# The low parts of the streamed weights on POOL: two instructions of half a tile each in place of one of the whole tile

## Chip, cores and metric

One Trainium2 chip, one of its cores. The metric is the device time of one execution in microseconds (us); lower is better. The times given are medians over runs of the whole kernel. The engines are called PE (matrix multiply; PEld is its weight load), DVE (vector), ACT (scalar), POOL (GpSimd) and SP (the queue that issues the DMAs).

## What is computed

One layer of a bidirectional encoder on 2048 positions of width 1024, in float32: an RMS norm, one projection into attention and state-space inputs, windowed attention beside a two-way state-space scan, an output projection, and a gated feed-forward block with a short convolution. By far the most arithmetic lies in the products with the weights:

```python
def reference(x, ...):
    for l in range(DEPTH):
        h = rmsnorm(x, norm1_g[l])
        proj = h @ w_in[l]
        q, k, v, z, xbc, dt_raw = jnp.split(proj, IN_SPLITS, axis=-1)
        attn = rmsnorm(windowed_attention(q, k, v, ...), attn_out_g[l])
        ssd = ssd_mixer(z, xbc, dt_raw, ...)
        x = x + jnp.concatenate([attn, ssd], axis=-1) @ w_out[l]
        h = rmsnorm(x, norm2_g[l])
        u = dwconv(h @ w_up[l], ffn_conv_w[l], ffn_conv_b[l])
        gate, val = jnp.split(u, 2, axis=-1)
        x = x + (jax.nn.silu(gate) * val) @ w_down[l]
    return rmsnorm(x, final_norm_g)
```

## The kernel before

Every large product is made of three matmuls on float32r operands, since one alone is too coarse: each operand is split into a high part `hi` (rounded to float32r) and a low part `lo` (the rest, `raw - hi`). `mm3` (lines 107 to 109) issues, for one 128 x 128 block of weights and one block of 512 positions, first `whi` with `xhi` (L107), then `whi` with `xlo` (L108), then `wlo` with `xhi` (L109). Only L109 reads the low part of the weights.

The weights stream through the core in 336 tiles of 128 partitions x 1024 columns (768 in some tiles of the down projection). A tile holds eight blocks of 128 columns, used one after the other: `up_mm` runs the eight blocks (index `k`) of one tile in turn, 24 matmuls in all; `wo_unit` does the same for the output projection; in `down_unit` the first half of the tile's columns belongs to one block of output rows and the second half to the next.

`next_w` keeps the stream two tiles ahead. For each tile, `w_raw` issues the DMA into `wraw`, and `w_split` makes `whi` with a copy on ACT (L142) and `wlo` with a subtraction that reads `wraw` and `whi` (L143). That subtraction runs on DVE for 24 tiles of the first stage (the first five and those listed in `WVS`) and on POOL for the other 312. `wraw`, `whi` and `wlo` have two buffers each, so tile i waits for the matmuls of tile i-2 to be done with theirs; for a few tiles `wplace` gives a place of their own (`wup`, `wdn`).

What else POOL does stands in the same queue: the low parts of some activation blocks (`split`, L209), sums of squares (L205), and steps of the state-space scan (L629, L631, L919, L941, L943), nearly all on 512 columns.

The stages: up to about 610 us the projections, scans and first attention blocks, in an order written out by hand (`PLAN`). Then four blocks `j` of 512 positions through the feed-forward part, the last one ending the kernel; beside each of the first three run attention and scan of the next block (`start_side`, `pace`), and between blocks stands the output projection (`wo_split` L991, `wo_x1`, `wo_unit`) with the norm stage `h2_stage`. The program text gives a first order. The builder then schedules the instructions by its own estimate of when each can run, and with that fixes the order of each engine's queue and the semaphore waits.

Of the kernel before, what the change touches and what calls it, by code (L numbers as in the profile page):

```python
# [10 lines left out]
F32 = mybir.dt.float32  # L11
F32R = mybir.dt.float32r
AF = mybir.ActivationFunctionType
ALU = mybir.AluOpType
# [22 lines left out]
WV = 5  # L37
PC = (1, 1, 1)
SQ_LAG = 7
WVS = (2, 3, 4, 6, 7, 9, 10, 12, 13, 14, 19, 21, 25, 26, 27, 28, 29, 31, 32, 33, 36, 40)  # L40
# [17 lines left out]
def block_kernel(ctx: ExitStack, tc: tile.TileContext, a: dict, out: bass.AP):  # L58
# [53 lines left out]
    V, G, A, T = nc.vector, nc.gpsimd, nc.scalar, nc.tensor  # L112
# [7 lines left out]
    def w_raw(i):  # L120
        if i >= len(wplan) or i in wraws:
            return
        src, m = wplan[i]
        raw = wpool.tile([P, 1024], F32, tag="wraw", name="wraw")
        dst = raw[:, :m]
        if len(src.shape) == 3:
            dst = dst.rearrange("p (i n) -> p i n", i=2)
        nc.sync.dma_start(dst, src)
        wraws[i] = raw

    def w_split(i):
        if i >= len(wplan) or i in wdone:
            return
        w_raw(i)
        m = wplan[i][1]
        raw = wraws[i]
        if i in wplace:
            hi, lo = wplace.pop(i)
        else:
            hi = wpool.tile([P, 1024], F32R, tag="whi", name="whi")  # L140
            lo = wpool.tile([P, 1024], F32R, tag="wlo", name="wlo")
        A.copy(hi[:, :m], raw[:, :m])  # L142
        (V if i < WV or i in WVS else G).tensor_tensor(lo[:, :m], raw[:, :m], hi[:, :m].bitcast(F32), ALU.subtract)  # L143
        wdone[i] = (hi, lo)

    def next_w():
        i = wpos[0]
        wpos[0] += 1
        w_split(i)
        w_raw(i + 1)  # L150
        w_split(i + 1)
        w_raw(i + 2)
        return wdone.pop(i)
# [1238 lines left out]
    for j in range(NB):  # L1392
# [5 lines left out]
        for g, (k0, nk) in enumerate(GROUPS):  # L1398
# [3 lines left out]
            i = 0  # L1402
            if j == 0 and g == 0 and UP2:
# [9 lines left out]
                i = 2  # L1413
# [118 lines left out]
```

## Time and profile before

| | before |
|---|---|
| median of 3 runs | 2447.28 us (2445.77 to 2447.74) |
| the profiled execution, device time | 2447.17 us |
| its span, first to last instruction | 2445.0 us |
| granted PE clock, mean | 0.986 of full speed |
| PE busy | 2344.5 us, 96% |
| DVE / ACT / POOL busy | 1666.2 / 1075.4 / 1091.7 us |

PE is the engine with the least idle time. Its busy time is that of overlapping instructions: a matmul of 512 columns is shown with some 0.39 us, while the next one starts 0.23 us after it. The idle time of the weight loads tells more plainly where PE had to stand. A row of the timeline gives start, duration, engine, line, operation, what is written and read, and in brackets the idle time before it and what ended it. Times are in us from the start of the span unless ns is said.

### The profile page before, as it was taken

How to read it: one execution, taken by the hardware profiler on the slowest of the kernel's cores; microseconds unless marked ns; L12 is line 12 of the kernel's file. 1: busy time of each engine (PE TensorE's matmuls, PEld its weight loads, DVE VectorE, ACT ScalarE, POOL GpSimd, SP SyncE). 2: the span in 40 equal slices, each digit the busy share in tenths (PEclk: the TensorE clock that was granted, in tenths of full speed). 3: DMA queues.
4: the chain of work that ended last, by engine and by line, in shares of the span. 5: the costliest groups of instructions: out<-in, count | busy, mean ns of one | idle time of the engine just before them, and what ended most of it. 6: DMA issues, size and time to landing. Idle time of an engine off the chain costs nothing.

```text
span 2445.0 us, 31146 instructions
## 1 busy us (share of the span) xinstructions
PE 2344.5 (96%) x11440; PEld 1955.9 (80%) x11440; DVE 1666.2 (68%) x2867; ACT 1075.4 (44%) x1818; POOL 1091.7 (45%) x585
## 2 busy tenths in 40 slices
PE   7999998897999999999999999999999999999997
PEld 6878797776788878777888887778888877888887
DVE  5756777687886784567877675688676566844445
ACT  5443565345454443435444444354444343433334
POOL 1014314464545544455454454555544445544444
PEclk9999999898999999999999999999999999999998
DMA  6466445883443433333444343244333232423232
GB/s 230 157 202 217 137 147 169 243 289 117 131 138 101 143 125 98 120 93 125 130 139 132 104 136 121 87 134 136 126 126 95 83 126 85 130 95 95 95 93 80
DMA packets 172459, 325.80 MB, mean 133 GB/s; under 512 B 12690, under 2 KB 83730, under 8 KB 172308
## 3 DMA queue, kind: packets, MB, share of 16 engines
q1 hardware_dynamic: 172308, 323.83, 41.5%
q8 instruction: 90, 1.47, 0.3%
q14 instruction: 61, 0.50, 0.1%
HBM read 277.77 MB, written 44.71 MB: 132 GB/s over the span
## 4 chain that ended last, share of the span: by engine, by line
PE 52%; DVE 7%; POOL 3%; DMA 1%; issue 1%; ACT 1%; DVEq 0%; POOLq 0%; ACTq 0%
PE up_b L109 10%; PE up_b L107 10%; PE up_b L108 10%; PE dn_b L107 3%; PE dn_b L109 3%; PE dn_b L108 3%; POOL wlo L143 2%; PE dn L109 2%; PE dn L108 2%; PE dn L107 2%; DVE m_lo L991 1%; PE wo_b L109 1%; DVE sm L777 1%; PE wo_b L108 1%; PE wo_b L107 1%
## 5 line engine op out<-in xcount | busy, mean ns | idle before, releaser
L143 POOL TENSOR_TENSOR wlo<-wraw,whi 128x1024 fp32r<-128x1024 f32 (+1 forms) x306 | 742.5, 2427 | 890.1 <-ACT whi L142 819.0
L142 ACT CAST whi<-wraw 128x1024 fp32r<-128x1024 f32 (+1 forms) x330 | 339.2, 1028 | 558.7 <-PE up_b L108 214.1
L109 PE MATMUL up_b<-h_hi,wlo 128*128 128x512 f32 x1392 | 550.4, 396 | 11.4 <-POOL wlo L143 11.4
L107 PE MATMUL up_b<-h_hi,whi 128*128 128x512 f32 x1392 | 552.0, 397 | 1.1 <-ACT h_hi L208 0.7
L108 PE MATMUL up_b<-h_lo,whi 128*128 128x512 f32 x1392 | 550.3, 396 | 1.9 <-DVE h_lo L209 1.9
L1066 DVE SCALAR_TENSOR_TENSOR fa<-up_b,fcw,fa 128x510 f32<-128x510 f32 (+2 forms) x396 | 271.2, 686 | 246.5 <-ACT fa L1068 242.3
L109 PEld LDWEIGHTS up_b<-h_hi,wlo 128*128 128x128 f32 x1392 | 262.3, 188 | 73.4 <-POOL wlo L143 15.4
L108 PEld LDWEIGHTS up_b<-h_lo,whi 128*128 128x128 f32 x1392 | 262.4, 188 | 59.7 <-DVE h_lo L209 3.5
L107 PEld LDWEIGHTS up_b<-h_hi,whi 128*128 128x128 f32 x1392 | 261.8, 188 | 59.1 <-ACT whi L142 1.2
L107 PE MATMUL dn_b<-f,whi 128*128 128x512 f32 x528 | 211.4, 400 | 1.1 <-DVE hal L1077 0.7
L108 PE MATMUL dn_b<-f,whi 128*128 128x512 f32 x528 | 209.0, 396 | 0.0
L109 PE MATMUL dn_b<-f,wlo 128*128 128x512 f32 x528 | 204.7, 396 | 0.0
L1068 ACT ACTIVATE fa<-up_b,fcw 128x512 f32<-128x512 f32 x176 | 135.9, 774 | 11.4 <-DVE fth L1089 11.1
L1116 DVE TENSOR_TENSOR x<-x,dn_b 128x512 f32<-128x512 f32 x144 | 97.7, 680 | 62.1 <-PE dn_b L109 61.6
L1087 ACT ACTIVATE fth<-fa 128x512 f32<-128x512 f32 (+1 forms) x88 | 55.6, 632 | 164.7 <-DVE fa L1079 115.6
L107 PEld LDWEIGHTS dn_b<-f,whi 128*128 128x128 f32 x528 | 99.7, 189 | 24.1 <-issue 2.1
L894 DVE SCALAR_TENSOR_TENSOR ab<-ab,ldt,mask 128x128 f32<-128x128 f32 x256 | 104.3, 475 | 19.0 <-DMA ab<-acs_d 19.0
L109 PEld LDWEIGHTS dn_b<-f,wlo 128*128 128x128 f32 x528 | 99.4, 188 | 21.9
L108 PEld LDWEIGHTS dn_b<-f,whi 128*128 128x128 f32 x528 | 99.2, 188 | 21.1
L1093 DVE TENSOR_TENSOR f<-fth,f 128x512 fp32r<-128x512 f32 (+1 forms) x88 | 105.7, 1201 | 14.4 <-ACT f L1092 13.5
L1092 ACT CAST f<-fth 128x512 fp32r<-128x512 f32 (+1 forms) x88 | 54.2, 616 | 107.9 <-DVE fth L1089 105.6
L107 PE MATMUL pj_b<-h_hi,whi 128*128 128x512 f32 x208 | 84.9, 409 | 15.1 <-ACT h_hi L236 6.8
(336 smaller groups left out, 4841.0 us busy)
## 6 DMA issues: line engine op xcount, KB each, us to landing
wraw<-in_w_up SPq DMA_DIRECT2D x176, 512.0 KB
wraw<-in_w_dn SPq DMA_DIRECT2D x64, 512.0 KB
wraw<-in_w_out SPq DMA_DIRECT2D x36, 512.0 KB
ab<-acs_d SPq DMA_DIRECT2D x32, 512.0 KB
wraw<-in_w_ch SPq DMA_DIRECT2D x28, 512.0 KB
wraw<-in_w_dn SPq DMA_DIRECT2D x32, 384.0 KB
ak<-ks_d SPq DMA_DIRECT2D x14, 768.0 KB
xt<-in_x SPq DMA_DIRECT2D x16, 512.0 KB
```

The source lines that it names most:

```text
L107: nc.tensor.matmul(ps, whi, xhi, start=first, stop=False)
L108: nc.tensor.matmul(ps, whi, xlo, start=False, stop=False)
L109: nc.tensor.matmul(ps, wlo, xhi, start=False, stop=last)
L142: A.copy(hi[:, :m], raw[:, :m])
L143: (V if i < WV or i in WVS else G).tensor_tensor(lo[:, :m], raw[:, :m], hi[:, :m].bitcast(F32), ALU.subtract)
L894: (G if i < SUBP[0 if first else 1] else V).scalar_tensor_tensor(ab[:, i, d], ab[:, i, d], ldt[:, d, c, h : h + 1], mask3[:, 2 * d * P : ( ...
L1066: V.scalar_tensor_tensor(o, src, w(q), o, ALU.mult, ALU.add)
L1068: A.activation(ai[:, 0:TB], u, AF.Identity, bias=w(3), scale=w(2))
L1087: A.activation(th[:, :n], acc[:, 0, :n], AF.Tanh)
L1092: A.copy(fs[:, idx, 0, :n], th[:, :n])
L1093: V.tensor_tensor(fs[:, idx, 1, :n], th[:, :n], fs[:, idx, 0, :n].bitcast(F32), ALU.subtract)
L1116: V.tensor_tensor(xv, xv, ps[i], ALU.add)
```

## The change

In `w_split`, the tiles whose low part is made on POOL get it in two subtractions, the first over the first half of the columns, the second over the second half (512 each, or 384 each where the tile has 768). Tiles on DVE, the ACT copy and the DMAs are as before.

```diff
         A.copy(hi[:, :m], raw[:, :m])
-        (V if i < WV or i in WVS else G).tensor_tensor(lo[:, :m], raw[:, :m], hi[:, :m].bitcast(F32), ALU.subtract)
+        if i < WV or i in WVS:
+            V.tensor_tensor(lo[:, :m], raw[:, :m], hi[:, :m].bitcast(F32), ALU.subtract)
+        else:
+            for q in range(2):
+                sl = slice(q * m // 2, (q + 1) * m // 2)
+                G.tensor_tensor(lo[:, sl], raw[:, sl], hi[:, sl].bitcast(F32), ALU.subtract)
         wdone[i] = (hi, lo)
```

## Rows read from the trace of the kernel before

**Rows 1.** Page: busy time, share of the span and instructions of each engine.
```profile
PE 2344.5 (96%) x11440; PEld 1955.9 (80%) x11440; DVE 1666.2 (68%) x2867; ACT 1075.4 (44%) x1818; POOL 1091.7 (45%) x585
```
**Rows 2.** Page: the chain that ended last, shares of the span by line.
```profile
PE up_b L109 10%; PE up_b L107 10%; PE up_b L108 10%; PE dn_b L107 3%; PE dn_b L109 3%; PE dn_b L108 3%; POOL wlo L143 2%; PE dn L109 2%; PE dn L108 2%; PE dn L107 2%; DVE m_lo L991 1%; PE wo_b L109 1%; DVE sm L777 1%; PE wo_b L108 1%; PE wo_b L107 1%
```
**Rows 3.** Page, costliest groups: busy us, mean ns, idle before, releaser.
```profile
L143 POOL TENSOR_TENSOR wlo<-wraw,whi 128x1024 fp32r<-128x1024 f32 (+1 forms) x306 | 742.5, 2427 | 890.1 <-ACT whi L142 819.0
...
L109 PEld LDWEIGHTS up_b<-h_hi,wlo 128*128 128x128 f32 x1392 | 262.3, 188 | 73.4 <-POOL wlo L143 15.4
L108 PEld LDWEIGHTS up_b<-h_lo,whi 128*128 128x128 f32 x1392 | 262.4, 188 | 59.7 <-DVE h_lo L209 3.5
```
**Rows 4.** Waits of the weight loads: us in total, times, longest.
```profile
PEld up_b L109 <- POOL wlo L143: 15.4, 10, 3.2
PEld sc L754 <- DVE mxs L756: 11.1, 9, 3.2
PEld pt L782 <- DVE pl L786: 9.2, 3, 3.6
...
PEld wo_b L109 <- POOL wlo L143: 6.8, 8, 2.0
```
**Rows 5.** Timeline, weight loads of L109 that waited.
```profile
1094.58 0.19 PEld L109 LDWEIGHTS up_b<-h_hi,wlo 128*128 128x128 f32 x1 [1.17 <-POOL wlo L143]
...
1102.19 0.19 PEld L109 LDWEIGHTS up_b<-h_hi,wlo 128*128 128x128 f32 x1 [1.79 <-POOL wlo L143]
```
**Rows 6.** Chain of waits in order of time (start, us, what), a block transition.
```profile
1025.86 8.00 DMA x<-in_xT
...
1038.79 0.50 PE wo_b L109
1039.29 0.23 PE wo_b L107
```
**Rows 7.** Durations on POOL, by form (mean ns) and by line (ns min/median/max).
```profile
L143 POOL TENSOR_TENSOR wlo<-wraw,whi 128x1024 fp32r<-128x1024 f32 x278 | 688.4, 2477 | 816.6 <-ACT whi L142 752.2 <-DVE x L1016 12.5 <-PE sc L755 12.1
...
L143 POOL TENSOR_TENSOR wlo<-wraw,whi x306: 1832/2406/4035, 59.7 to 2403.4; 128x1024 fp32r<-128x1024 f32 x139, 128x768 fp32r<-128x768 f32 x14
...
L209 POOL TENSOR_TENSOR h_True_lo<-xb,h_True_hi x8: 1283/1313/1768, 235.0 to 262.0; 128x512 fp32r<-128x512 f32 x8
```
**Rows 8.** Timeline: a first matmul with a tile still being written.
```profile
2053.70 0.39 PE L108 MATMUL up_b<-h_lo,whi 128*128 128x512 f32 x1
...
2058.11 1.31 POOL L209 TENSOR_TENSOR h_lo<-h2t,h_hi 128x512 fp32r<-128x512 f32 x1 [1.28 <-ACT h_hi L208]
```
**Rows 9.** Durations on DVE, by line, by form, and one row of the timeline.
```profile
L777 DVE TENSOR_SCALAR sm<-sm,rsm x96: 346/415/2595, 571.4 to 1894.7; 128x384 f32<-128x384 f32 x88, 128x256 f32<-128x256 f32 x8
...
L777 DVE TENSOR_SCALAR sm<-sm,rsm 128x384 f32<-128x384 f32 x88 | 74.0, 893 | 0.5
...
L1066 DVE SCALAR_TENSOR_TENSOR fa<-up_b,fcw,fa x396: 205/748/754, 653.0 to 2397.3; 128x510 f32<-128x510 f32 x153, 128x511 f32<-128x511 f32 x23, 128x1 f32<-128x1 f32 x22
...
1021.69 2.88 DVE L991 SCALAR_TENSOR_TENSOR m_lo<-mixed,gv,m_hi 128x512 fp32r<-128x512 f32 x1
```
**Rows 10.** Timeline, POOL and DVE side by side.
```profile
1175.86 3.13 POOL L143 TENSOR_TENSOR wlo<-wraw,whi 128x1024 fp32r<-128x1024 f32 x1 [8.25 <-ACT whi L142]
1178.94 1.10 POOL L631 TENSOR_TENSOR statef<-statef,etot 128x512 f32<-128x512 f32 x1
...
1177.24 1.90 DVE L894 SCALAR_TENSOR_TENSOR ab<-ab,ldt,mask 128x128 f32<-128x128 f32 x1
...
1179.06 1.13 DVE L894 SCALAR_TENSOR_TENSOR ab<-ab,ldt,mask 128x128 f32<-128x128 f32 x1
```
**Rows 11.** Timeline: PE's order within one group of three matmuls.
```profile
1203.86 0.40 PE L108 MATMUL up_b<-h_lo,whi 128*128 128x512 f32 x1
...
1204.10 0.27 PE L818 MATMUL apr<-ident,arc 128*128 128x128 f32 x1
...
1204.13 0.48 PE L109 MATMUL up_b<-h_hi,wlo 128*128 128x512 f32 x1
```

## The prediction, made before the result was known

> **What bounds the kernel now.** I read the page's busy shares first: PE has work in 96% of the span, every other engine in less than 70% [rows 1]. PE is the bound, so a change elsewhere pays only where PE stands. The chain that ended last says by whose work PE is reached late: besides PE's own lines the largest entry is POOL's `wlo` on L143 with 2% of the span, some 49 us, then DVE's `m_lo` and `sm` with 1% each, some 24 us each [rows 2]. A share of the chain is not yet a loss, for PE may have been only just late. The loss stands in the waits of the weight loads: those of L109 waited for `wlo` 15.4 us in 10 places of the up projection and 6.8 us in 8 of the output projection, together 22.2 us in 18 stalls, the longest 3.2 us [rows 4]. That is 0.9% of the span and the most that an earlier `wlo` can return directly. The other waits of PE that bear on this are those for DVE: 11.1 us for `mxs`, 9.2 us for `pl` [rows 4].
>
> POOL itself is at 45% [rows 1]; the low parts take 742.5 us of it, and 819.0 of the 890.1 us idle before them ends with the ACT copy of `whi` [rows 3]. So as a rule POOL waits for its input and is late only where other work of its queue, or a late ACT copy, came in between. Of 312 tiles on POOL only some 18 are late for PE; the others have slack, and an earlier or later `wlo` changes nothing there.
>
> **Part 1, the first half comes earlier (the gain).** A `wlo` of 1024 columns takes 2.41 us in the median, 2.48 in the mean; the same subtraction on 512 columns (`h_True_lo`, float32r out as here) takes 1.31 us in the median, 1.28 at the least [rows 7]. PE needs only the first 128 columns of `wlo` for its first L109. If the wait goes by the half, the first L109 of a tile starts 2.41 - 1.31 = 1.10 us earlier.
>
> Does it go by the half? The trace of before shows a tile that is written in pieces: a matmul of L108 on `h_lo` runs at 2053.70, and POOL writes a piece of the same `h_lo` at 2058.11 [rows 8]. So the waits follow the region that an instruction touches, not the whole tile.
>
> When is the second half due? Its first reader is block 4 of the tile, 12 matmuls behind the first L109; at 0.23 us from one matmul to the next [rows 6] that is 2.76 us. It is ready 1.31 us behind the first half, or some 2.0 us if a DVE instruction of 0.7 us gets in between. It is hidden with 0.7 us to spare.
>
> Now the 18 stalls one by one in the timeline: eleven are over 1.1 us and add to 19.1 us, seven are below 0.7 us and add to 3.1 us; two of the eleven are shown [rows 5]. An earlier first half takes 1.10 us from each of the eleven, 12.1 us, and the whole of the seven, 3.1 us: 15.2 us. One deduction: the two shown, 7.6 us apart, repeat in the next block, and in such a pair the second `wlo` stands behind POOL's `h_lo`, whose time PE does not set. What PE gains at the first stall it waits for at the second, so one 1.10 of each pair is lost: 15.2 - 2.2 = **13.0 us gained**. Bounds: 15.2 if the pairs do add, 6.5 (half) if other work is next late.
>
> **Part 2, more waits on PE (at nothing).** Each of the 312 tiles gets a second semaphore wait, on the weight load of block 4. Of the weight loads of the up projection, those of L109 hold the waits for POOL; they take 188 ns like those of L108, and their idle time without the waits named is 73.4 - 15.4 = 58.0 us against 59.7 - 3.5 = 56.2 us over 1392 loads each [rows 3]. The difference is 1.8 us for some 170 satisfied waits, so at most 3 us for 312. A load overlaps the matmul before it, which is the cover; I take 0 and keep 3 for the range.
>
> **Part 3, POOL works longer (a cost).** Two halves take 2 x 1.31 = 2.62 us against 2.41: 0.21 us a tile, 66 us over 312 tiles. If POOL's 2.48 us mean is mostly waiting for DVE at the start, a pair may meet it twice, 0.07 us more. POOL goes from 45% to some 48% of the span; what is queued behind a `wlo` (scan steps, `h_lo`, the next `wlo`) starts 0.2 us later. On the path this counts only where the chain holds a whole `wlo` with more POOL work behind it, as at 1175.86 with `statef` behind [rows 10]. The 49 us of the chain [rows 2] are some 20 tiles, most of them those that PE waits for at once. I take 10 tiles at 0.21: **2 us lost**; bounds 0 and 6 (20 tiles at 0.28).
>
> [...]
>
> **Part 4, DVE is held for less (a gain of unsure size).** DVE's `sm` (L777) has a median of 415 ns but a mean of 893 and a maximum of 2595, that is, its own time plus the length of a `wlo` [rows 9]. `m_lo` took 2.88 us in one row, while L1066, of the same kind and width but fed from PSUM, never took over 754 ns [rows 9]. The place is plain at 1177.24: a small DVE instruction stays 1.90 us, until the `wlo` of 1175.86 ends at 1178.99, and the next stays 1.13 us, until `statef` ends [rows 10]. So a DVE instruction that takes its inputs from SBUF is held while POOL runs one, and POOL's next instruction goes ahead of DVE's next but one. Half of `sm` is such time, some 13 us of its 24 on the chain; for `m_lo` I take the same, 12 us. Halves help a DVE instruction that comes during the first half (one in two): it is let in 1.1 us earlier. If another such one follows at once, the second half holds that one instead, and nothing is won. A quarter of 25 us would be 6; since PE's own waits for DVE here are only 20.3 us [rows 4], **4 us gained**. Bounds: half, 12, and below zero 2 us lost, since a pair is 8% longer than one whole.
>
> [...]
>
> **The sum.** 13.0 + 4 - 2 = 15 us less. The profiled execution took 2447.17 us, with a span of 2445.0 and 2.2 around it; the median shown is 2447.28, the same within 0.1 us. So 2447.2 - 15 = **2432 us**, -0.6%. From the bounds its own range is 2421 to 2442 (15.2 + 12 gained and 1 lost; 13 gained, 2 lost on DVE and 6 on POOL).
>
> **Rivals.**
> (a) The gain is absorbed: PE arrives earlier and stands at the next late thing. For it: 8.00 us of `x<-in_xT` stand on the chain at 1025.86, before the output projection's stall at 1038.79 [rows 6], and DVE paces much of what comes before. Against it: at the 18 stalls it was `wlo` that came last, and the stretches between are PE's own. With half of part 1 and parts 3 and 4 in balance: -6.5, 2441 us.
> (b) The change does not do what it says: L109 waits for both halves after all. Then every stall is longer by 0.21, 18 x 0.21 = 4 us lost, 2 lost on POOL, 4 gained on DVE: 2449 us. Against it stands the `h_lo` written in pieces [rows 8].
> (c) Slower: other POOL work gets between the two halves. The queues are not in the order of the text: a transpose of the attention stands between the second and third matmul of one group [rows 11]. 312 more instructions with other times are scheduled anew. The place is the three blocks with scan steps beside the up projection, as around 1175 [rows 10]. The second half is due 2.76 us behind the first; with one POOL step of 1.3 us and one DVE hold of 0.7 in between it comes at 3.3 and PE stands 0.5 us, with two steps 1.9 us, on average 1.2. From 13 such tiles on the gain of 15 us is gone; with two in each of the 12 scan chunks of these blocks, 24 x 1.2 = 29 us, it is 2461 us. Nothing in the rows shows such an order, but nothing excludes it.
>
> **How the numbers follow.** About 0.2% (5 us) is what a measurement of this kernel can tell from no change. The forecast has 0.54, all of it faster. Rival (a), 2437 to 2446, has 0.22, of which 0.09 are faster by more than 5 us and 0.13 not. Rival (b) has 0.07, no change. Rival (c) has 0.17, slower. Together: faster 0.63, same 0.20, slower 0.17. The range goes from 2418 (the forecast's own low end and 3 us more, for reordering may also help) to 2452, which takes in (a) and (b) and leaves most of (c) out.
>
> **What the profile of the changed kernel would show.** Right: the waits of L109's weight loads for `wlo` fall from 22 to about 8 us, with hardly any at block 4; 624 POOL instructions on L143 with a median near 1.3 us and POOL busy near 1160 us; the mean of `sm` well below 893 ns. Part 1 is wrong if the stalls stay with the releaser being the second half (b), or if PE's idle time before other lines grows by what L109's falls (a). Rival (c) shows as stalls of L109 released by second halves, with other POOL work between the two. What would upset all of it is a visibly different order of PE's queue, with new stalls at lines that this change does not touch.

## The result, and the profile after

The changed kernel takes **2421.11 us** (median of 4 runs, 2418.16 to 2425.67) against 2447.51 us before (4 runs, 2445.77 to 2449.55): 26 us less, and by the estimate over the runs a ratio of 0.9898 [0.9882, 0.9913]. 2432 was forecast, with a range from 2418 to 2452: the sign and the range hold, and the forecast gain of 15 us is too small by 11; the measured time lies at the low end that the prediction's own bounds gave, 2421. The profiled execution of after is its slowest, 2425.67 us with a span of 2423.9. The traces below therefore show 21.1 of the 26 us.

The page of after: busy time, share and instructions of each engine, the chain that ended last by line, and three of the costliest groups (busy us, mean ns, idle before, releaser).

```profile
PE 2341.8 (97%) x11440; PEld 1958.3 (81%) x11440; DVE 1572.2 (65%) x2867; ACT 1076.3 (44%) x1818; POOL 1164.1 (48%) x897
...
PE up_b L109 11%; PE up_b L108 11%; PE up_b L107 11%; PE dn_b L108 5%; PE dn_b L107 5%; PE dn_b L109 5%; POOL wlo L148 2%; PE wo_b L109 2%; PE wo_b L108 2%; PE wo_b L107 2%; PE dn L108 1%; PE dn L107 1%; PE dn L109 1%; PE pt L787 1%; DVE ab L899 1%
...
L148 POOL TENSOR_TENSOR wlo<-wraw,whi 128x512 fp32r<-128x512 f32 (+1 forms) x612 | 815.4, 1354 | 812.0 <-ACT whi L142 757.6
...
L109 PEld LDWEIGHTS up_b<-h_hi,wlo 128*128 128x128 f32 x1392 | 261.6, 188 | 63.7 <-POOL wlo L148 6.9
L108 PEld LDWEIGHTS up_b<-h_lo,whi 128*128 128x128 f32 x1392 | 261.6, 188 | 59.6 <-DVE h_lo L214 3.4
```

Against [rows 1], POOL has 312 more instructions and 72.4 us more work. DVE has the same 2867 instructions and 94.0 us less busy time, although the change adds, removes or alters no DVE instruction. That second difference is the larger surprise of the page; part of it will turn out to belong to the order of the instructions and not to the halves. On the chain, DVE's `m_lo` and `sm`, 1% each in [rows 2], are no longer among the listed lines, and PE's own lines have grown (up projection from 10 to 11% a line, down projection from 3 to 5%). Against [rows 3], the idle time of L109's loads behind `wlo` has fallen from 15.4 to 6.9 us.

The waits of the weight loads after (us in total, times, longest):

```profile
PEld sc L759 <- DVE mxs L761: 9.5, 9, 3.2
PEld pt L787 <- DVE pl L791: 7.4, 3, 4.0
PEld up_b L109 <- POOL wlo L148: 6.9, 9, 1.9
PEld wo_b L109 <- POOL wlo L148: 4.7, 6, 1.1
PEld pj_b L107 <- DVE cu L337: 3.5, 2, 3.2
```

Two rows of the same view of before that [rows 4] does not show:

```profile
PEld pj_b L107 <- DVE cu L332: 7.0, 2, 3.9
PEld po L792 <- DVE pl L786: 3.8, 5, 1.4
```

The two rows on `wlo`, 22.2 us in 18 stalls in [rows 4], are now 11.6 us in 15. In the timeline each of these 15 is released by the first half of its tile, none by the second. The rows for DVE have fallen as well: `mxs` from 11.1 to 9.5, `pl` from 9.2 to 7.4 [rows 4], `cu` from 7.0 to 3.5. Over all lines, the gaps of over 0.1 us before weight loads add to 122.6 us before and 99.6 after (0.044 us, the usual step, taken off each). Of these 23.0 us, 10.9 lie at `wlo` and 12.1 elsewhere, 10.7 of them at loads that wait for DVE (51.2 us before, 40.5 after). So the traces already say that half of the gain is not at the line that the change was aimed at.

Durations after, on POOL and DVE (lines of the source: ns min/median/max; groups by form: busy us, mean ns):

```profile
L148 POOL TENSOR_TENSOR wlo<-wraw,whi x612: 1007/1297/2342, 62.1 to 2383.1; 128x512 fp32r<-128x512 f32 x139, 128x384 fp32r<-128x384 f32 x14
...
L782 DVE TENSOR_SCALAR sm<-sm,rsm x96: 345/417/1484, 572.3 to 1878.8; 128x384 f32<-128x384 f32 x88, 128x256 f32<-128x256 f32 x8
L782 DVE TENSOR_SCALAR sm<-sm,rsm 128x384 f32<-128x384 f32 x88 | 51.9, 643 | 0.4
L996 DVE SCALAR_TENSOR_TENSOR m_lo<-mixed,gv,m_hi x36: 473/804/1780, 522.7 to 1966.3; 128x512 fp32r<-128x512 f32 x28, 128x256 fp32r<-128x256 f32 x8
```

Two halves take 2 x 1.297 = 2.594 us in the median against 2.406 [rows 7]. The longest `sm` went from 2595 to 1484 ns and the mean from 893 to 643 [rows 9]. The longest `m_lo` went from 2887 ns (first row below) to 1780: what it has over the median fell from 2.15 us (740 ns) to 0.98 (804 ns), as a tile's 2.41 us on POOL became a half's 1.30.

The same place in both traces, the output projection's `m_lo` beside two tiles of low parts. The line's durations before, and the timeline of before (start, us, what):

```profile
L991 DVE SCALAR_TENSOR_TENSOR m_lo<-mixed,gv,m_hi x36: 469/740/2887, 521.6 to 1986.4; 128x512 fp32r<-128x512 f32 x28, 128x256 fp32r<-128x256 f32 x8
...
1018.58 5.44 POOL L143 TENSOR_TENSOR wlo<-wraw,whi 128x1024 fp32r<-128x1024 f32 x2 [4.67 <-ACT whi L142]
...
1019.62 4.96 DVE L991 SCALAR_TENSOR_TENSOR m_lo<-mixed,gv,m_hi 128x512 fp32r<-128x512 f32 x2
```

and of after:

```profile
1016.51 6.58 POOL L148 TENSOR_TENSOR wlo<-wraw,whi 128x512 fp32r<-128x512 f32 x4 [4.08 <-ACT whi L142]
...
1017.48 2.76 DVE L996 SCALAR_TENSOR_TENSOR m_lo<-mixed,gv,m_hi 128x512 fp32r<-128x512 f32 x2
1020.16 0.68 DVE L1121 TENSOR_TENSOR x<-x,dn_b 128x512 f32<-128x512 f32 x1
1020.76 1.19 DVE L996 SCALAR_TENSOR_TENSOR m_lo<-mixed,gv,m_hi 128x512 fp32r<-128x512 f32 x1
```

The median `m_lo` of before takes 0.74 us. Two of them beside two whole tiles took 4.96 us; two beside halves took 2.76, and DVE then made another `x` and a third `m_lo` while the third and fourth half ran. Taken one by one, each of these five `m_lo` ends 0.55 us behind the end of the POOL instruction beside it. So at this place DVE gets its turn at each end of a POOL instruction, and there are now twice as many ends. The price is on POOL, whose four halves take 6.58 us against 5.44.

One more thing differs between the traces: the builder scheduled anew. Matched by line, operation, tiles and shape, 10716 of PE's 11440 instructions stand in the same order before and after (the longest such sequence), on DVE 2561 of 2867, on ACT 1681 of 1818. So three causes were possible: the earlier first half (part 1), shorter holds of DVE (part 4), and another order.

### The profile page after: what moved, and what is told of

Read it like the earlier page. It is cut to its first block, busy times and chain, and to the rows that moved or that the text cites. A ratio compares the mean times of both kernels' runs of the same rounds, so it can differ in the third digit from the quotient of the medians.

```text
span 2423.9 us, 31674 instructions
## 1 busy us (share of the span) xinstructions
PE 2341.8 (97%) x11440; PEld 1958.3 (81%) x11440; DVE 1572.2 (65%) x2867; ACT 1076.3 (44%) x1818; POOL 1164.1 (48%) x897
## 4 chain that ended last, share of the span: by engine, by line
PE 64%; DVE 5%; POOL 3%; issue 2%; DMA 1%; ACT 1%; DVEq 0%; POOLq 0%; ACTq 0%
PE up_b L109 11%; PE up_b L108 11%; PE up_b L107 11%; PE dn_b L108 5%; PE dn_b L107 5%; PE dn_b L109 5%; POOL wlo L148 2%; PE wo_b L109 2%; PE wo_b L108 2%; PE wo_b L107 2%; PE dn L108 1%; PE dn L107 1%; PE dn L109 1%; PE pt L787 1%; DVE ab L899 1%
## 5 line engine op out<-in xcount | busy, mean ns | idle before, releaser
L148 POOL TENSOR_TENSOR wlo<-wraw,whi 128x512 fp32r<-128x512 f32 (+1 forms) x612 | 815.4, 1354 | 812.0 <-ACT whi L142 757.6
L107 PE MATMUL up_b<-h_hi,whi 128*128 128x512 f32 x1392 | 551.1, 397 | 0.8 <-DVE hal L1082 0.4
L109 PE MATMUL up_b<-h_hi,wlo 128*128 128x512 f32 x1392 | 547.7, 394 | 3.6 <-POOL wlo L148 3.3
L108 PE MATMUL up_b<-h_lo,whi 128*128 128x512 f32 x1392 | 548.1, 394 | 2.6 <-DVE h_lo L214 2.6
L109 PEld LDWEIGHTS up_b<-h_hi,wlo 128*128 128x128 f32 x1392 | 261.6, 188 | 63.7 <-POOL wlo L148 6.9
L108 PEld LDWEIGHTS up_b<-h_lo,whi 128*128 128x128 f32 x1392 | 261.6, 188 | 59.6 <-DVE h_lo L214 3.4
L107 PEld LDWEIGHTS up_b<-h_hi,whi 128*128 128x128 f32 x1392 | 261.0, 188 | 59.3 <-ACT whi L142 2.2
L107 PE MATMUL dn_b<-f,whi 128*128 128x512 f32 x528 | 210.9, 400 | 0.0
L108 PE MATMUL dn_b<-f,whi 128*128 128x512 f32 x528 | 209.0, 396 | 0.0
L109 PE MATMUL dn_b<-f,wlo 128*128 128x512 f32 x528 | 207.4, 396 | 0.0
L899 DVE SCALAR_TENSOR_TENSOR ab<-ab,ldt,mask 128x128 f32<-128x128 f32 x256 | 104.2, 474 | 32.4 <-DMA ab<-acs_d 32.4
L109 PEld LDWEIGHTS dn_b<-f,wlo 128*128 128x128 f32 x528 | 99.3, 188 | 22.4
L107 PEld LDWEIGHTS dn_b<-f,whi 128*128 128x128 f32 x528 | 99.8, 189 | 21.4
L108 PEld LDWEIGHTS dn_b<-f,whi 128*128 128x128 f32 x528 | 99.3, 188 | 21.1
L107 PE MATMUL pj_b<-h_hi,whi 128*128 128x512 f32 x208 | 86.3, 416 | 11.9 <-ACT h_hi L241 6.7
L761 DVE CUSTOM_DVE_ANT_0 sm<-sc,mask,vecs 128x384 f32<-128x384 f32 (+1 forms) x116 | 66.4, 597 | 46.3 <-PE sc L760 45.1
```

Of the source, the lines that this page charges most:

```text
L107: nc.tensor.matmul(ps, whi, xhi, start=first, stop=False)
L108: nc.tensor.matmul(ps, whi, xlo, start=False, stop=False)
L109: nc.tensor.matmul(ps, wlo, xhi, start=False, stop=last)
L148: G.tensor_tensor(lo[:, sl], raw[:, sl], hi[:, sl].bitcast(F32), ALU.subtract)
L761: V.tensor_tensor_reduce(sm[kv][i][:, :n], sc[:, :n], mask3[:, m0 : m0 + n], 0.125, sink[:, h : h + 1], ALU.add, ALU.max, mxs[kv][:, i : i ...
L899: (G if i < SUBP[0 if first else 1] else V).scalar_tensor_tensor(ab[:, i, d], ab[:, i, d], ldt[:, d, c, h : h + 1], mask3[:, 2 * d * P : ( ...
```

## The experiments

Each time is compared with that of the kernel before in the same group of runs: 2446.37, 2447.02, 2446.02 and 2445.22 us in the four groups. All kernels compute the whole reference.

**Was it the order?** Two kernels take the order of every engine's queue from another version and keep it, whatever the durations. The version is scheduled first, and then each instruction is tied behind its forerunner of that queue, an order without a semaphore; further pieces of a tile stand right behind its first. (The helper moves the later lines. In the pinned kernels below, `wlo` on POOL is L157 or L158, L116 or L117 is L107 of before, and L118 or L119 is L109; where a listing names L107, L109 and L148, it is a kernel without the helper, as after.)

```diff
+            for queue in order:
+                made = [i for p in queue for i in places[p]]
+                for a, b in zip(made, made[1:]):
+                    tc.add_manual_dep(b, a.name, info, reason="issue order")
...
+PARTS = [1]
+MINE = 2
+ORDER_OF = 1
```

That is the first, halves in the order of the kernel before; the second, whole tiles in the order of the changed kernel, has `MINE = 1` and `ORDER_OF = 2`. In their traces PE and ACT issue every instruction in the order asked for, and DVE all but one in the first.

> Two halves per tile as in the change, but every engine's queue keeps the order of the kernel before (the schedule of the kernel before is computed first and pinned by order-only edges). Theory A (the halves themselves make the gain: earlier first half, DVE held for less; order without part): 2420 to 2425 us, as the changed kernel. Theory B (forecast's own terms are right, 15 us, and the new order of the queues brings the other 11): 2432 us. Theory C (most of the gain is the new order): 2440 us or more.

Measured: 2420.25 us, 0.9891 [0.9876, 0.9906].

> One whole subtraction per tile as before, every queue pinned to the order of the changed kernel. Theory A: as before, 2447 us. Theory B: 2436 us. Theory C: 2428 us or less.

Measured: 2451.83 us, 1.0027 [1.0017, 1.0037]. The changed kernel itself ran beside these two.

> The changed kernel once more, timed beside the three others on the same chip: 2421 us, the comparison for the rest.

Measured: 2421.47 us, 0.9893 [0.9879, 0.9906]. Halves gain 26.1 us in the old order and 24.9 in the new. The new order alone, with whole tiles, costs 5.5. So the gain is that of the halves; the new order has no share in it. The pages of the first two of these kernels:

```profile
PE 2335.4 (97%) x11440; PEld 1956.7 (81%) x11440; DVE 1578.3 (65%) x2867; ACT 1076.7 (45%) x1818; POOL 1173.6 (49%) x897
...
PE 2350.7 (96%) x11440; PEld 1963.7 (80%) x11440; DVE 1632.0 (67%) x2867; ACT 1076.2 (44%) x1818; POOL 1085.1 (44%) x585
```

DVE's busy time is 87.9 us less with halves in the old order. But it is also 34.2 us less with whole tiles in the new order, in a kernel that is slower than before: a shorter busy time of DVE alone is not yet a gain. The later questions on the halves were therefore put in the old order, where nothing else moves.

**Which tiles, and which part?** The first kernel cuts only the 20 tiles for which PE had waited in the trace of before (18 of the up and output projections, 2 others). The second cuts only the other 292, for which PE did not wait in that trace, so that part 1 should bring nothing there. (The kernel with reversed halves, shown third, ran before these two; their expectations use its 2433.9 us.)

```diff
+LATE = (38, 84, 102, 105, 116, 117, 130, 154, 178, 180, 181, 192, 193, 206, 254, 256, 257, 268, 280, 335)
+LATE_ONLY = lambda i, m: HALVES(i, m) if i in LATE else WHOLE(i, m)
+ALL_BUT_LATE = lambda i, m: WHOLE(i, m) if i in LATE else HALVES(i, m)
+MINE = LATE_ONLY
+ORDER_OF = WHOLE
```

> Order of the kernel before; halves only for the 20 tiles whose low part PE waited for in the profile of before, the other 292 POOL tiles whole. If the earlier first half works by these stalls alone: 13 to 14 us less than before, 2433 us, which is what the reversed halves lacked against the halves (2433.9 against 2420.3). If the gain needs all tiles: 2440 us or more.

Measured: 2431.83 us, 0.9938 [0.9926, 0.9950], 15.2 us less. Its waits of weight loads for `wlo`, and its `sm`:

```profile
PEld up_b L118 <- POOL wlo L157: 5.7, 6, 2.2
PEld wo_b L118 <- POOL wlo L157: 1.5, 2, 1.1
...
L792 DVE TENSOR_SCALAR sm<-sm,rsm 128x384 f32<-128x384 f32 x88 | 74.1, 894 | 0.5
```

The stalls fall as far as in the changed kernel and further (22.2 to 7.2 us), while `sm` stays where it was (893). This is part 1 nearly by itself: DVE's busy time is 1653.0 us, 13.2 less than before, where two executions of the changed kernel differ by 7.0 (1572.2 and 1579.2).

> Order of the kernel before; halves for the 292 POOL tiles that PE did not wait for, whole for the 20. The first half of these tiles is early for nobody, so what it gains is the shorter hold of DVE less POOL's longer work: 2434 us if the reversed halves' gain of 12 us was that; 2445 us or more if it was something of the reversed order itself.

Measured: 2435.16 us, 0.9955 [0.9940, 0.9969], 11.9 us less.

```profile
PEld up_b L118 <- POOL wlo L157: 14.5, 7, 3.1
PEld sc L769 <- DVE mxs L771: 7.8, 6, 3.2
PEld pt L797 <- DVE pl L801: 7.7, 3, 4.5
PEld wo_b L118 <- POOL wlo L157: 6.1, 6, 2.1
PEld pj_b L116 <- DVE cu L347: 3.6, 2, 3.2
...
PEld po L807 <- DVE pl L801: 2.4, 3, 1.0
...
L792 DVE TENSOR_SCALAR sm<-sm,rsm 128x384 f32<-128x384 f32 x88 | 47.5, 591 | 0.5
```

(The profiled execution is the fastest of the six, 2430.93 us, so the rows show some 4 us more than the median gained.) The reverse picture: `wlo` still costs 20.6 us, `sm` is down to 591 ns, and most of what PE gains it gains at lines that wait for DVE. The four rows on `mxs`, `pl` (two lines) and `cu` fall from 11.1 + 9.2 + 3.8 + 7.0 = 31.1 us before to 7.8 + 7.7 + 2.4 + 3.6 = 21.5. The two kernels share no cut tile and their gains add: 15.2 + 11.9 = 27.1 against the 26.1 of all tiles.

The second test of the same question keeps every cut and takes the early half away. POOL makes the second half of the columns first, so the columns that PE wants first come last.

```diff
+REVERSED = lambda i, m: [(m // 2, m), (0, m // 2)]
+MINE = REVERSED
```

> Order of the kernel before; two halves, but the second half of the columns is made first, so that the first matmul on the low part waits for both (2.62 us instead of 2.41). What is left of the change is that DVE is held for less and POOL works longer. If the earlier first half is most of the gain: 2447 to 2452 us. If the shorter hold of DVE brings as much as the forecast's 4 us or more: 2440 to 2445 us.

Measured: 2433.90 us, 0.9946 [0.9934, 0.9959], 12.5 us less.

```profile
PEld up_b L118 <- POOL wlo L157: 17.1, 11, 3.7
PEld wo_b L118 <- POOL wlo L157: 5.9, 5, 1.7
```

Now the stalls at these two lines are 23.0 us, not less than the 22.2 before, and still half of the gain is there. Against the right sequence of halves it is 13.6 us slower, which is part 1 again. The time is below both bands of the expectation, whose lower one began at 2440: what is left without the early half was taken too small here too. Over all rows of this view (as listed, nothing taken off), the loads wait for POOL 30.7 us before, 16.1 with only the late tiles cut, 28.1 with all but these and 32.1 reversed; for DVE it is 53.3, 52.1, 43.6 and 39.7. The two parts show on different engines.

**How small may the pieces be?** Four and eight pieces per tile, in the old order (the cut is that of eight; four has the same with `QUARTERS`):

```diff
+EIGHTHS = lambda i, m: [(q * m // 8, (q + 1) * m // 8) for q in range(8)]
+MINE = EIGHTHS
+ORDER_OF = WHOLE
```

> Order of the kernel before; four pieces of 256 columns. A piece should take some 0.73 us, four 2.9 us. If the hold of DVE goes on shrinking with the length of a POOL instruction and the first piece comes 0.55 us earlier still: 2410 to 2416 us. If in dense runs every piece holds one DVE instruction and POOL's 0.3 us a tile more is felt: 2421 us or more.

Measured: 2414.64 us, 0.9865 [0.9849, 0.9881], the fastest of all. Its page, its pieces on POOL (ns min/median/max) and its wait for `wlo`, from an execution of 2409.1 us:

```profile
PE 2332.7 (97%) x11440; PEld 1956.1 (81%) x11440; DVE 1525.8 (63%) x2867; ACT 1077.8 (45%) x1818; POOL 1294.0 (54%) x1521
...
L158 POOL TENSOR_TENSOR wlo<-wraw,whi x1224: 591/742/2359, 61.6 to 2366.7; 128x256 fp32r<-128x256 f32 x159, 128x192 fp32r<-128x192 f32 x16
...
PEld up_b L119 <- POOL wlo L158: 2.9, 4, 1.3
```

> Eight pieces of 128 columns in the order of before. POOL then takes some 8 x 0.47 = 3.8 us a tile and is busy near 65%. If the shorter hold goes on paying: 2405 to 2412 us. If POOL's longer work takes over (PE waits again for later pieces, scan steps late): 2418 us or more.

Measured: 2424.18 us, 0.9911 [0.9897, 0.9925].

```profile
PE 2340.7 (97%) x11440; PEld 1955.8 (81%) x11440; DVE 1495.5 (62%) x2867; ACT 1077.2 (44%) x1818; POOL 1502.8 (62%) x2769
...
L158 POOL TENSOR_TENSOR wlo<-wraw,whi 128x128 fp32r<-128x128 f32 (+1 forms) x2448 | 1161.1, 511 | 556.5 <-ACT whi L152 504.6
...
L158 POOL TENSOR_TENSOR wlo<-wraw,whi x2448: 382/463/2079, 62.7 to 2381.7; 128x128 fp32r<-128x128 f32 x172, 128x96 fp32r<-128x96 f32 x17
...
PEld up_b L119 <- POOL wlo L158: 6.2, 11, 2.1
...
PEld wh_b L119 <- DVE wlo L154: 4.3, 3, 3.1
...
PEld dn_b L119 <- POOL wlo L158: 1.8, 4, 0.5
```

With one, two, four and eight pieces the time is 2446, 2420, 2415 and 2424 us, DVE's busy time falls all the way (1666, 1578, 1526, 1496) and POOL's rises (1092, 1174, 1294, 1503). At eight, a tile takes 8 x 0.511 = 4.1 us of POOL, and stalls for `wlo` come back: in the up projection, and in the down projection (`dn_b`), where there are none with four; a tile made on DVE (`wh_b`) is later too, 4.3 against 1.9 us. Over all rows of that view the waits for POOL go from 11.8 us with four to 19.5 with eight, those for ACT from 35.3 to 39.6 and for DVE from 35.0 to 38.6. So the fall of DVE's busy time no longer reaches PE, and POOL's own work is the largest part of what is lost; the rest was not taken apart.

**The copy in halves too?** The first half of `wlo` could start earlier if ACT's copy came in halves as well.

```diff
-        A.copy(hi[:, :m], raw[:, :m])
...
+                A.copy(hi[:, sl], raw[:, sl])
```

> The changed kernel, in its own order, with the ACT copy of the high part of the POOL tiles in two halves as well, each ahead of its half on POOL. The first half then starts some 0.4 us earlier, at 0.2 us more of ACT per tile. If the stalls of PE for the low part that are left (11 us in 15 places) go by that: 2415 to 2418 us. If ACT is late for other things: 2421 us or more.

Measured: 2435.74 us, 0.9956 [0.9942, 0.9970], in an order of its own, some 14 us slower than the changed kernel's 2421.47 us in another group. Whether this is the copy or the order, the next one tells:

> Halves on POOL and halves of the ACT copy for the same tiles, every queue in the order of the kernel before. If the copy in halves itself is what made that kernel slow (2435.7): 2430 us or more. If it was only the order that the builder made: 2415 to 2420 us, as the halves in the old order (2420.3) or a little better.

Measured: 2418.57 us, 0.9881 [0.9865, 0.9898]. In the old order the copy in halves costs nothing; nor can a gain be told from the 0.9891 of halves with a whole copy. Set against the kernel before, the two runs of it stand 11.3 and 27.5 us lower; the 16 us between them are the order's.

**What is an order worth?** Quarters as a change of the text alone (`range(4)`, scheduled anew), and whole tiles in the order that the builder made for those quarters (`MINE = WHOLE`, `ORDER_OF = QUARTERS`):

> Four pieces per tile in the program text alone, with the order of the queues that the builder then makes of it. If the order has little part, as with the halves: 2412 to 2417 us, as the quarters in the order of before (2414.6). If a new order costs what the halves of the copy showed (2435.7 against 2421.5): 2425 us or more.

Measured: 2430.31 us, 0.9933 [0.9920, 0.9947]. Its waits:

```profile
PEld wo_b L107 <- ACT whi L142: 10.7, 3, 4.1
PEld up_b L109 <- POOL wlo L148: 4.0, 4, 1.6
```

> One whole subtraction per tile as in the kernel before, every queue pinned to the order that the builder made for the four pieces. If that order by itself costs the 16 us that lie between the quarters in it (2430.3) and in the old order (2414.6): 2460 us or more. If the order only hurts together with the pieces: 2447 us.

Measured: 2468.26 us, 1.0094 [1.0080, 1.0108].

```profile
PEld up_b L119 <- POOL wlo L158: 19.0, 17, 3.0
PEld wo_b L117 <- ACT whi L152: 14.8, 3, 5.8
PEld wo_b L119 <- POOL wlo L158: 10.2, 6, 1.9
```

This order alone costs 23.0 us, and quarters in it are 15.7 us better than before where they are 32.4 in the old order. The new stall is the same in both kernels: loads of the output projection wait for ACT's copy, 10.7 and 14.8 us in three places (3.0 us with quarters in the old order). That is a cost of the order, not of the pieces. Why the builder puts the copies there was not looked into.

A stall is not all that an order costs. In the trace of this kernel PE's granted clock falls to 0.5 of full speed during each of the three stalls for the copy (4.5, 5.8 and 4.5 us long), and stays there for 10.2, 6.8 and 6.8 us. Over all runs the granted clock is 0.9798 in the mean, against 0.9859 of the kernel before beside it; as an estimate, (1 - clock) times the span, that is 15 of the 23 us. For whole tiles in the order of the halves it is 0.9840 against 0.9865, some 6 us, as much as that order costs. The gain of the halves is not of this kind: in the old order they have 0.9865, as the kernel before. For the other kernels in the old order the same estimate gives 1 to 6 us of their gains, 1 for all but the late tiles and 5 for the quarters.

## Why the prediction was right, and where it was too small

**Part 1, the earlier half: right.** 13.0 us were forecast, 15.2 measured where only the late tiles are cut (with what little these 20 bring on DVE), and 13.6 between the two sequences of halves. The whole estimate, 15.2 before the deduction for pairs, lies as near. The interval of the ratio, some 3 us to either side, can't say whether the pairs lose their 2.2. The waits go by the half: 15 stalls of after end with the first half, and rival (b) is out.

**Part 2, more waits on PE: right at nothing.** L109's idle time without `wlo` is 63.7 - 6.9 = 56.8 us after, L108's without `h_lo` 59.6 - 3.4 = 56.2. The 0.6 us between them is no more than the 1.8 us of before. That a load overlaps the matmul before it is seen in the trace of before: a load of L109 starts at 1115.22, while the matmul of 1114.99 runs until 1115.38.

**Part 3, POOL's longer work: right in size.** 72.4 us more on POOL, forecast 66; the median of a half 1.297 us, forecast near 1.3; POOL at 1164.1 us, forecast 1160. What it costs PE was not isolated. It is contained in the 11.9 and 12.5 us of the two kernels that show part 4, so the two terms are compared as a net. Two halves against one whole give 0.19 us a tile (2.594 - 2.406), where the forecast took 0.21 from the rows.

**Part 4, DVE held for less: the term that was mis-sized.** Parts 4 and 3 together were forecast at 4 - 2 = 2 us gained; they gain 11.9 (all but the late tiles) and 12.5 (reversed, which also pays for later first columns). That is some 10 of the 11 us by which the forecast missed; part 1 can account for the rest. The mechanism was right and the size was not: the bound of 12 took it in, the value of 4 did not. Three steps to that value failed:
- The cap. Part 4 was held down because PE's waits for DVE were only 20.3 us. That took two rows of the view. With `cu` and the second line of `pl` the same view of before has 31.1 us, and 9.6 of these went in the kernel that cuts only tiles PE did not wait for. All its rows for DVE add to 53.3.
- The base. It was reckoned from the 25 us of `sm` and `m_lo` on the chain. But other lines are held too: the page has 94.0 us less busy time after (87.9 with halves in the old order), and `sm` accounts for 74.0 - 51.9 = 22.1 of the 94.0. Not all are: L1066, fed from PSUM, never took over 754 ns [rows 9].
- The dense run. That "the second half holds that one instead, and nothing is won" is refuted by the `m_lo` rows above: in a dense run too, the hold lasts as long as the POOL instruction, and a shorter instruction holds for less: two `m_lo` took 4.96 us beside two whole tiles and 2.76 beside halves.

That less DVE busy time comes with smaller POOL pieces is shown, by one, two, four and eight pieces in one order. That POOL's instruction is what holds DVE's is read from durations tied to POOL's ends (each of the five `m_lo` above ends 0.55 us behind one); what the two share is not shown, and no run took a shared access away. How much of DVE's time PE gets back is not given by the sum either: 87.9 us less on DVE went with some 12 us.

**Rivals.** (a), absorbed at 2441, is out: PE's waits fell elsewhere too, and the parts add. (c) did not come by its mechanism: in none of the 312 pairs does other POOL work stand between the halves, and the second half ends 1.26 us behind the first in the median and 2.30 at most, where 2.76 were allowed. But its premise, that a new order can cost more than the change brings, is real: the order of this change costs 5.5 us with whole tiles, that of quarters 23.0. By the estimate above, much of that lies in the granted clock, for which the prediction has no term. In this change the halves outweigh it; 2421.5 with the new order and 2420.3 with the old can't be told apart.

The prediction's signs: waits for `wlo` "about 8 us", 11.6 in the profile of after (7.2 with only the late tiles cut); no stall at block 4; `sm` below 893 ns, 643. The sign that should have upset everything, a different order of PE's queue with new stalls at other lines, came by half: the order differs, and the stalls elsewhere are shorter in sum.

## What to carry to other kernels

Where POOL and DVE both read SBUF for much of the time, as here, the length of one POOL instruction can be a delay that DVE meets again and again (an `m_lo` with a median of 0.74 us took up to 2.89 with whole tiles, one with 0.80 up to 1.78 with halves): look at the maximum and mean of a DVE line beside its median, and take all of PE's waits for DVE as the room for a gain, not two of its lines. DVE's busy time shows that it is held for less, not what that is worth: with eight pieces it is lowest and the kernel is not the fastest. Stop cutting where POOL's added time per piece (here some 0.2 us) makes its own results late; here that was between four and eight. And when a builder reorders the queues with each edit, pin the order before comparing, and look at the granted clock beside the stalls: the best version here, quarters in the old order (2414.6 us), looks 16 us worse when its text is simply compiled.

## What the runs showed that was not expected

In one order, cutting POOL's instructions makes DVE's total busy time shorter in every step, by 87.9 us with halves and by 1666.2 - 1495.5 = 170.7 with eight pieces, with not one DVE instruction changed. And the price of a piece on POOL is steady: pieces of 128, 256, 512 and 1024 columns take 0.463, 0.742, 1.297 and 2.406 us in the median (a few narrower ones among them), that is 2.17 ns for each of the columns and 0.19 us for each instruction. Last, the order that came with a small edit cost up to 23 us by itself, by the estimate above mostly through PE's granted clock.
